# PEER feed-forward on one core: raw-weight ring in spent operand buffers, more GpSimd subtractions, a lighter backlog, and another first expert group

## The chip, the cores and the metric

One core of one Trainium2 chip. The metric is the device time of one execution in microseconds, taken as the median of several runs. Lower is better.

## The reference

Two transformer blocks run one after the other over 256 tokens of width 2048. The first block and the mixer of the second (two kinds of attention with gated branches) are not touched. The change lies in the last part, the product-key feed-forward (PEER):

```python
def peer_ffn(h, w_query, sub_keys, expert_u, expert_v):
    q = (ht @ w_query).reshape(n_tok, PEER_HEADS, 2, HALF_KEY)
    scores = jnp.einsum('thpc,hpnc->thpn', q, sub_keys)
    s1, i1 = lax.top_k(scores[:, :, 0], PEER_TOPK)
    s2, i2 = lax.top_k(scores[:, :, 1], PEER_TOPK)
...
    top_score, pos = lax.top_k(cand_score, PEER_TOPK)
    expert_ids = jnp.take_along_axis(cand_id, pos, axis=-1)
    gates = jax.nn.softmax(top_score, axis=-1)
...
        act = jax.nn.gelu(jnp.einsum('thkd,td->thk', expert_u[idb], xb))
        return jnp.einsum('thk,thkd->td', gb * act, expert_v[idb])
```

There are 8 heads with 16 chosen experts each, out of 128 x 128 = 16384 experts. `h` is `x` after an RMS norm, and a last residual addition and RMS norm follow.

## The kernel before

**Dense products instead of gathers by token.** The kernel multiplies all 256 tokens with all 16384 rows of `expert_u` (the *first expert product*), applies gelu, and multiplies by a gate matrix that is zero where an expert was not chosen. The result, `a`, goes to DRAM (`a_dram`, one row of 256 tokens for each expert). The last stage multiplies `a` with rows of `expert_v`.

**Weight units.** All big products read their weights as 332 *units* of [128, 2048] f32. Units 188 to 203 are the queries' weights (`wq`), units 204 to 331 the first expert product (`uT`), 32 chunks of 4 units. Each unit goes through a pipeline:

- SyncE's queue (SP) issues two loads of [128, 1024] into `raw`, a pool of four such tiles (`load_half`, L102);
- ScalarE rounds a half to `wh` (L111);
- VectorE, or GpSimd for the pairs (unit, half) in the table `POOL_SUB`, computes `wl = raw - wh` (L112);
- TensorE multiplies with `wh` and `wl` (L216 and L217, L213 and L214 for the edges of an accumulation). Two units are half of a chunk, and each half ends in an epilogue that ScalarE starts (L225) and VectorE adds to (L226).

`pump` sets the order: before unit n it records the loads up to unit n + 2 and the splits up to unit n + 1. The `raw` tile of a half comes free when both ScalarE and the engine of the subtraction have read it.

**Side work.** Generators (`side`) are advanced four times in a unit, between the matmuls of the product:

- `topk_a` (L1114 to L1140) makes scores and finds the top 16 on VectorE. Until the gates exist, chunks of the first product are spilled to DRAM (`xs`, L1243); 19 are.
- `g_build` (L1300 to L1329) builds the gate matrix out of one-hot rows `oh`, and writes it to `g_dram`.
- `order_experts` (L1395 to L1494) sorts the experts so that unused ones come together. It makes 16 pairs of one-hot matrices (`ob` L1479, `oa` L1483, both VectorE; `ob` is scaled by ScalarE, L1480) and 128 small matmuls (L1490). Its result is the index `idx` of the gathers in the last stage.
- `backlog` brings the spilled chunks back: a gate load `G` (L1354), a load of the chunk `Xr` (L1359), a multiply on VectorE (L1368) and a write to `a_dram` (L1371) for each chunk, with 6 yields behind it.

**Last stage.** 64 groups of 256 experts are taken in the order `gro`, which starts 55, 14, 37, ... For a group, GpSimd issues two gathers of [128, 2048] from `expert_v` (`v_load`, tiles `vraw`, six of them, L1532) and two of [128, 256] from `a_dram` (`a_load`, `araw`, L1538). `v_split` makes `ah` and `al` from `araw` (L1544, L1545), then `vh` and `vl` (L1552, L1553). The matmuls (L1561 to L1563) stand under conditions on the number of experts used, so a group of unused experts costs TensorE nothing. L1561 runs 648 times in the profiled execution, 8 for each of 81 pairs of a group and a half of the tokens, and the groups are sorted; of the first group, 55, none runs.

The operands of the products live in a pool `hbr` of tiles [128, 2048]: the queries' operand `act3` takes four, the expert product's operand `act4` four more. `act3` is last read by unit 203.

Of the kernel before, what the change touches and what calls it, by code (L numbers as in the profile page):

```python
# [6 lines left out]
F32 = mybir.dt.float32  # L7
F32R = mybir.dt.float32r
# [4 lines left out]
AF = mybir.ActivationFunctionType  # L13
# [33 lines left out]
TB = 32  # L47
GW = 8
GB = 3
POOL_SUB = {(n, 1) for n in [*range(8, 24, 2), *range(36, 64, 2), *range(188, 332, 2)]}  # L50
PRIO = 1000
EPRIO = 6000
OHB = 12
# [12 lines left out]
def model(tc, I, out):  # L66
    nc = tc.nc
    V, S, T, PO = nc.vector, nc.scalar, nc.tensor, nc.gpsimd
    es = ExitStack()
    with es:  # L70
        cpool = es.enter_context(tc.tile_pool(name="cst", bufs=1))
        es_w = es.enter_context(ExitStack())
        rawp = es_w.enter_context(tc.tile_pool(name="raw", bufs=NRAW))
        whp = es_w.enter_context(tc.tile_pool(name="wh", bufs=NWH))
        wlp = es_w.enter_context(tc.tile_pool(name="wl", bufs=NWL))
        hbr = es_w.enter_context(tc.tile_pool(name="hbr", bufs=8))
# [15 lines left out]

        units = []
        raws, splits, hooks = {}, {}, {}
        pos = [0, 0, 0]
        active, waiting = [[], []], [[], []]

        def load_half(n, hf, parts=1):
            f = rawp.tile([128, 1024], F32, name="raw", tag="raw")
            w = units[n][0][:, hf * 1024:(hf + 1) * 1024]  # L100
            for i in range(0, 1024, 1024 // parts):
                nc.sync.dma_start(f[:, i:i + 1024 // parts], w[:, i:i + 1024 // parts])  # L102
            raws.setdefault(n, []).append(f)
# [42 lines left out]
        def pump(upto):  # L146

            while pos[2] < upto:
                n = pos[2]
                while pos[0] < min(len(units), n + 3):  # L150
                    with tc.high_priority(offset=PRIO):
                        load(pos[0])
                    pos[0] += 1
                while pos[1] < min(len(units), n + 2, pos[0]):
                    with tc.high_priority(offset=PRIO):
                        split(pos[1])
                    pos[1] += 1
                units[n][1](splits.pop(n))
                pos[2] += 1
                for f in hooks.pop(pos[2], []):  # L160
                    f()
# [175 lines left out]
        def rB(R, n=4):  # L337
            return R[:, None, 0:256].to_broadcast([128, n, 256])
# [6 lines left out]
        with ExitStack() as b1:  # L345
            w_ = b1.enter_context(tc.tile_pool(name="work1", bufs=1))
# [439 lines left out]
            for u in range(4):  # L786
                t = H("xr")
                xr.append(t)
                if u < 2:
                    f = rawp.tile([128, 1024], F32, name="raw", tag="raw")  # L790
                    h, l = whp.tile([128, 1024], F32R, name="wh"), wlp.tile([128, 1024], F32R, name="wl")
# [89 lines left out]
            late = []  # L881
# [217 lines left out]
        with ExitStack() as bt:  # L1099
# [8 lines left out]

            def q_epi(c):
                def epi(q):  # L1110
                    V.tensor_mul(q, q, rB(R3))
                    for t in range(2):
                        side(topk_a(c, t, q))
                return epi  # L1114

            def topk_a(c, t, q):

                p = sps()
                for j in range(4):
                    hp = c * 4 + j  # L1120
                    T.matmul(p[:, j * 128:j * 128 + 128], q[:, j, t * 128:t * 128 + 128],
                             skT[hp // 8][:, (hp % 8) // 2, (hp % 2) * 128:(hp % 2) * 128 + 128],
                             start=True, stop=True)
                yield
                sc = small("sc", [128, 4, 128], bufs=2)
                sc2 = small("sc2", [128, 4, 128], bufs=SC2)
                S.activation(sc, p.rearrange("p (a b) -> p a b", a=4), AF.Copy)
                yield
                ix = small("ix", [128, 4, 16], bufs=2, dt=U32)
                for j in range(4):  # L1130
                    sv = s12[t][:, c * 4 + j]
                    V.max(sv[:, 0:8], sc[:, j])
                    V.max_index(ix[:, j, 0:8], sv[:, 0:8], sc[:, j])
                    V.match_replace(sc2[:, j], sv[:, 0:8], sc[:, j], -3e38)
                    V.max(sv[:, 8:16], sc2[:, j])
                    V.max_index(ix[:, j, 8:16], sv[:, 8:16], sc2[:, j])
                    yield
                V.tensor_copy(x12[t][:, c * 4:c * 4 + 4], ix)
                done.append((c, t))
                if sum(1 for d in done if d[1] == t) == 4:  # L1140
                    side(topk_b(t))
                yield
# [125 lines left out]
                gemm(I["wq"][c], act3, 4, q_epi(c))  # L1268
            side(scaled())
            n = len(units) + 1  # L1270
            for c in range(NS):
                gemm(I["uT"][c], act4, 4, u_epi(c), parts=c == NS - 1)
            while len(ready) < 2:
# [100 lines left out]
        def backlog(sets):  # L1374
            for i, c in enumerate(sets):
                if i == 0:
                    load_g(c)
                    load_x(c)
                yield
                if i + 1 < len(sets):  # L1380
                    load_g(sets[i + 1])
                    load_x(sets[i + 1])
                make_a(c)
                for _ in range(6):
                    yield

        def order_experts():
# [131 lines left out]
        NV = 12  # L1519
        NGR = NT // KG  # L1520
        gro = [(i * 23 + 55) % NGR for i in range(NGR)]
        raw, ar, sv, sa = {}, {}, {}, {}

        def ix(i, kk):
# [3 lines left out]
        def v_load(i):  # L1528
            raw[i] = []
            for kk in range(KG):  # L1530
                f = w_.tile([128, 2048], F32, name="vraw", tag="vraw", bufs=6)
                PO.indirect_dma_start(f, None, I["v"], ix(i, kk))  # L1532
                raw[i].append(f)

        def a_load(i):
            ar[i] = w_.tile([128, KG, 256], F32, name="araw", tag="araw", bufs=4)
            for kk in range(KG):
                PO.indirect_dma_start(ar[i][:, kk], None, arow, ix(i, kk))  # L1538

        def v_split(i):  # L1540
            h = w_.tile([128, KG, 256], F32R, name="ah", tag="ah", bufs=3)
            l = w_.tile([128, KG, 256], F32R, name="al", tag="al", bufs=3)
            f = ar.pop(i)
            S.activation(h, f, AF.Copy)  # L1544
            V.tensor_sub(l, f, h.bitcast(F32))  # L1545
            sa[i] = (h, l)
            sv[i] = []
            for f in raw.pop(i):
                for hf in range(2):
                    q = slice(hf * 1024, hf * 1024 + 1024)  # L1550
                    h, l = (w_.tile([128, 1024], F32R, name=n, tag=n, bufs=NV) for n in ("vh", "vl"))
                    S.activation(h, f[:, q], AF.Copy)  # L1552
                    V.tensor_sub(l, f[:, q], h.bitcast(F32))  # L1553
                    sv[i].append((h, l))

        def v_mm(i, t, last=False):
            ah, al = (x[:, :, t * 128:t * 128 + 128] for x in sa[i])
# [17 lines left out]
        es_d.enter_context(order_)  # L1575
        for i in range(3):
            v_load(i)
            a_load(i)
        s1, e0, e1 = (T.value_load(bnd[0:1, i:i + 1], min_val=0, max_val=NT * 128) for i in range(3))
        for i in range(2):  # L1580
            v_split(i)
        v_load(3)
        a_load(3)
        for i in range(NGR):
# [151 lines left out]
```

## Time and profile before

| | us |
|---|---|
| median of 3 runs | 2651.11 (2650.2 to 2661.93) |
| the profiled execution's own time | 2651.99 |
| its span | 2650.2 |
| TensorE busy | 2546.2 (96%) |
| VectorE busy | 1947.1 (73%) |
| ScalarE busy | 1492.9 (56%) |
| GpSimd busy | 662.7 (25%) |

The shares are means over the whole program, and its stages differ: units 188 to 203 run from about 1220 to 1310 us, the first expert product from there to 2150, and the last stage from 2150 to the end. The granted clock of TensorE was 0.987 over the span. The profile of the chain that ended last is of no help in this program: TensorE is almost always the one that ends last, and what matters is where it stands still.

### The profile page before, as it was taken

Reading aid. Unit: us, or ns where it says so; the run is one execution under the profiler, and the core shown is the slowest. Engines: PE = TensorE matmul, PEld = TensorE weight load, DVE = VectorE, ACT = ScalarE, POOL = GpSimd, SP = SyncE. Lnnn points to the kernel's source line nnn. Section 1 sums busy time; section 2 is a strip of 40 time slices with the busy share of each in tenths; the row PEclk is TensorE's granted clock in tenths of the full one; section 3 lists DMA queues with packets and bytes.
Section 4 is the critical chain, followed back from the end, with each engine's and each line's share of the span. In section 5 each row is a group of like instructions: output and inputs, shape, how many; then the busy total and the mean of one; then the engine's idle time right before and its main releaser. Section 6 shows DMA issues by size and latency. Waiting matters only on the chain. (4 is left out here: it accounts for less than half of the span.)

```text
span 2650.2 us, 38662 instructions
## 1 busy us (share of the span) xinstructions
PE 2546.2 (96%) x14650; PEld 2166.0 (82%) x14650; DVE 1947.1 (73%) x2691; ACT 1492.9 (56%) x2179; POOL 662.7 (25%) x401
## 2 busy tenths in 40 slices
PE   8999999999999999999998999999799989999998
PEld 7878878888888888888887788888687867777776
DVE  7988877675555655767999888888975447767776
ACT  7666665555544544555455777664453446656565
POOL 0440111000000000001214221221211248667773
PEclk9999999999999999999999999999899989999999
DMA  6454424554555455555555677778799769898885
GB/s 226 154 170 154 158 97 137 201 179 158 175 169 173 165 185 185 188 190 192 175 184 175 214 232 233 231 234 299 264 353 347 239 237 360 305 330 317 320 311 209
DMA packets 173397, 584.81 MB, mean 221 GB/s; under 512 B 17424, under 2 KB 50704, under 8 KB 156688
## 3 DMA queue, kind: packets, MB, share of 16 engines
q1 hardware_dynamic: 114192, 411.88, 45.5%
q0 software_dynamic: 24576, 151.01, 15.6%
q10 hardware_dynamic: 34432, 19.27, 2.5%
q8 instruction: 126, 2.06, 0.3%
q14 instruction: 71, 0.58, 0.1%
HBM read 536.48 MB, written 45.61 MB: 220 GB/s over the span
## 5 line engine op out<-in xcount | busy, mean ns | idle before, releaser
L216 PE MATMUL acc<-a,wh 128*128 128x512 f32 x3120 | 1121.6, 401 | 3.6 <-ACT wh L111 2.7
L111 ACT ACTIVATE wh<-raw 128x1024 fp32r<-128x1024 f32 x662 | 696.7, 1056 | 481.8 <-PE acc L216 256.8
L112 DVE TENSOR_TENSOR wl<-raw,wh 128x1024 fp32r<-128x1024 f32 x568 | 722.0, 1275 | 300.0 <-ACT wh L111 296.7
L217 PE MATMUL acc<-a,wl 128*128 128x256 f32 x3120 | 886.5, 284 | 26.9 <-DVE wl L112 15.2
L216 PEld LDWEIGHTS acc<-a,wh 128*128 128x128 f32 x3120 | 590.4, 189 | 135.3 <-ACT wh L111 4.3
L112 POOL TENSOR_TENSOR wl<-raw,wh 128x1024 fp32r<-128x1024 f32 x94 | 268.6, 2857 | 1692.4 <-ACT wh L111 1634.8
L217 PEld LDWEIGHTS acc<-a,wl 128*128 128x128 f32 x3120 | 594.8, 191 | 37.6 <-DVE wl L112 19.9
L1553 DVE TENSOR_TENSOR vl<-vraw,vh 128x1024 fp32r<-128x1024 f32 x256 | 296.5, 1220 | 14.9 <-ACT vh L1552 14.4
L1561 PE MATMUL o<-vh,ah 128*128 128x512 f32 x648 | 257.3, 397 | 28.8 <-ACT vh L1552 11.9
L216 PE MATMUL acc<-ax,wh 128*128 128x512 f32 x720 | 266.4, 407 | 10.6 <-ACT wh L800 6.5
L1562 PE MATMUL o<-vl,ah 128*128 128x512 f32 x648 | 253.5, 391 | 0.5 <-DVE vl L1553 0.5
L1563 PE MATMUL o<-vh,al 128*128 128x512 f32 x648 | 253.2, 391 | 0.0
L1552 ACT ACTIVATE vh<-vraw 128x1024 fp32r<-128x1024 f32 x256 | 248.9, 1044 | 0.0
L225 ACT ACTIVATE y<-acc 128x512 f32<-128x512 f32 x162 | 96.0, 593 | 226.0 <-PE acc L214 224.1
L217 PE MATMUL acc<-ax,wl 128*128 128x256 f32 x720 | 209.7, 291 | 5.2 <-DVE wl L112 3.0
L226 DVE TENSOR_TENSOR y<-y,acc 128x512 f32<-128x512 f32 x162 | 110.6, 683 | 128.4 <-ACT y L225 127.8
L1532 POOL DMA_INDIRECT vraw<-in_v_dram,idx x128 | 165.1, 1290 | 86.5 <-DVE vl L1553 50.7
L1538 POOL DMA_INDIRECT araw<-a_dram,idx x128 | 174.6, 1364 | 48.2 <-issue 36.9
L1561 PEld LDWEIGHTS o<-vh,ah 128*128 128x128 f32 x648 | 122.2, 189 | 68.4 <-issue 26.7
L216 PEld LDWEIGHTS acc<-ax,wh 128*128 128x128 f32 x720 | 138.9, 193 | 40.2 <-ACT wh L800 6.5
L217 PEld LDWEIGHTS acc<-ax,wl 128*128 128x128 f32 x720 | 139.6, 194 | 8.9 <-DVE wl L112 3.9
L1544 ACT ACTIVATE ah<-araw 128x512 fp32r<-128x512 f32 x64 | 40.3, 629 | 188.9 <-PE o L1562 139.6
(508 smaller groups left out, 3716.6 us busy)
## 6 DMA issues: line engine op xcount, KB each, us to landing
raw<-in_w_dram SPq DMA_DIRECT2D x278, 512.0 KB, 4.2
raw<-in_uT_dram SPq DMA_DIRECT2D x256, 512.0 KB, 4.9
raw<-in_wo_dram SPq DMA_DIRECT2D x64, 512.0 KB, 4.4
raw<-in_wq_dram SPq DMA_DIRECT2D x32, 512.0 KB, 4.2
g_dram<-gst ACTq DMA_DIRECT2D x32, 512.0 KB, 7.7
G<-g_dram SPq DMA_DIRECT2D x32, 512.0 KB, 7.3
xs<-y SPq DMA_DIRECT2D x19, 512.0 KB, 4.5
Xr<-xs SPq DMA_DIRECT2D x19, 512.0 KB, 9.9
```

What stands on the lines that cost most here:

```text
L111: S.activation(h[:, q], f[:, q], AF.Copy)
L112: (PO if (n, hf) in POOL_SUB else V).tensor_sub(l[:, q], f[:, q], h[:, q].bitcast(F32))
L216: T.matmul(acc[:, j], wh[:, js], xx, start=f, stop=False)
L217: T.matmul(acc[:, j, 0], wl[:, js], xx[:, 0], start=False, stop=False)
L226: V.tensor_add(y, y, acc[:, :, 0])
L1532: PO.indirect_dma_start(f, None, I["v"], ix(i, kk))
L1538: PO.indirect_dma_start(ar[i][:, kk], None, arow, ix(i, kk))
L1552: S.activation(h, f[:, q], AF.Copy)
L1553: V.tensor_sub(l, f[:, q], h.bitcast(F32))
L1561: T.matmul(ps[t][d], ah[:, kk], wh, start=False, stop=False)
L1562: T.matmul(ps[t][d], ah[:, kk], wl, start=False, stop=False)
L1563: T.matmul(ps[t][d], al[:, kk], wh, start=False, stop=stop)
```

## The change

It has six parts. In the changed file the lines stand 6 to 12 further down.

1. From unit 208 on, the raw weights go to four tiles of a whole unit each, out of `hbr` (`ring`, the tiles of `act3`), and the loads run up to unit n + 4.
2. `POOL_SUB` gets the second halves of the odd units 189 to 223 as well: 18 more subtractions on GpSimd instead of VectorE.
3. The queries' scale `R3`, a VectorE multiply in each of four epilogues (L1111), becomes the scale of the ScalarE copy of the scores (L1127).
4. `backlog` yields 7 times behind a chunk instead of 6.
5. `gro[0]` and `gro[7]` change places: group 24 is now the first, group 55 the eighth.
6. In the last stage the first three `v_load` are issued ahead of the first three `a_load`, and the first group's `ah` and `al` are made behind its `vh` and `vl`.

```diff
-POOL_SUB = {(n, 1) for n in [*range(8, 24, 2), *range(36, 64, 2), *range(188, 332, 2)]}
+POOL_SUB = {(n, 1) for n in [*range(8, 24, 2), *range(36, 64, 2), *range(188, 224), *range(224, 332, 2)]}
...
         def load_half(n, hf, parts=1):
-            f = rawp.tile([128, 1024], F32, name="raw", tag="raw")
+            if ring and n >= ring[0]:
+                if len(ring) == 1:
+                    ring.extend(hbr.tile([128, 2048], F32, name="ring", tag="hbr") for _ in range(4))
+                f = ring[1 + n % 4][:, hf * 1024:(hf + 1) * 1024]
+            else:
+                f = rawp.tile([128, 1024], F32, name="raw", tag="raw")
...
-                while pos[0] < min(len(units), n + 3):
+                while pos[0] < min(len(units), n + (5 if len(ring) > 1 else 3)):
...
                 def epi(q):
-                    V.tensor_mul(q, q, rB(R3))
...
-                S.activation(sc, p.rearrange("p (a b) -> p a b", a=4), AF.Copy)
+                S.activation(sc, p.rearrange("p (a b) -> p a b", a=4), AF.Copy, scale=R3[:, 256 + t:257 + t])
...
             n = len(units) + 1
+            ring.append(len(units) + 4)
...
                 make_a(c)
-                for _ in range(6):
+                for _ in range(7):
                     yield
...
         gro = [(i * 23 + 55) % NGR for i in range(NGR)]
+        gro[0], gro[7] = gro[7], gro[0]
...
         for i in range(3):
             v_load(i)
+        for i in range(3):
             a_load(i)
...
         for i in range(2):
-            v_split(i)
+            v_split(i, late=i == 0)
```

On SyncE's queue, where the first expert product's loads begin, this stood before (`raw` are the half tiles, `xs` the spilled chunks):

```order
L102 DMA raw<-in_wq_dram 128x1024 x32
L102 DMA raw<-in_uT_dram 128x1024 x15
L1243 DMA xs_13235<-y 128x1024
L102 DMA raw<-in_uT_dram 128x1024 x8
L1243 DMA xs_13496<-y 128x1024
```

and this stands there now:

```order
L108 DMA raw<-in_wq_dram 128x1024 x32
L108 DMA raw<-in_uT_dram 128x1024 x3
L108 DMA ring<-in_uT_dram 128x1024 x2
L108 DMA raw<-in_uT_dram 128x1024 x2
L108 DMA ring<-in_uT_dram 128x1024 x4
L108 DMA raw<-in_uT_dram 128x1024 x2
L108 DMA ring<-in_uT_dram 128x1024 x2
L108 DMA raw<-in_uT_dram 128x1024
L108 DMA ring<-in_uT_dram 128x1024 x4
L1248 DMA xs_13235<-y 128x1024
L108 DMA ring<-in_uT_dram 128x1024 x8
```

The first loads into the ring have moved ahead of five of the eight halves of units 204 to 207 on the same queue, and they need the matmuls of the last query units to be done. From there on each load goes to a ring tile, up to two units earlier than before.

On VectorE, in the stretch of `order_experts`, this stood before (unit 289 and the next ones; `ob` and `oa` are the one-hots, `y<-y,acc` is an epilogue):

```order
L112 TENSOR_TENSOR wl<-raw,wh 128x1024
L1479 TENSOR_TENSOR ob<-cst,pf 128x1024
L1483 TENSOR_TENSOR oa<-cst,pf 128x1024
L1479 TENSOR_TENSOR ob<-cst,pf 128x1024
L1483 TENSOR_TENSOR oa<-cst,pf 128x1024
L1468 CAST jf<-ji 128x128
L112 TENSOR_TENSOR wl<-raw,wh 128x1024
L226 TENSOR_TENSOR y<-y,acc 128x512
```

and this stands at the beginning of the one-hots now (unit 293 and the next ones; L1374 is the backlog's multiply):

```order
L1485 TENSOR_TENSOR ob<-cst,pf 128x1024
L1489 TENSOR_TENSOR oa<-cst,pf 128x1024
L118 TENSOR_TENSOR wl<-ring,wh 128x1024
L232 TENSOR_TENSOR y<-y,acc 128x512
L118 TENSOR_TENSOR wl<-ring,wh 128x1024 x2
L1485 TENSOR_TENSOR ob<-cst,pf 128x1024
L1489 TENSOR_TENSOR oa<-cst,pf 128x1024
L118 TENSOR_TENSOR wl<-ring,wh 128x1024
L232 TENSOR_TENSOR y<-y,acc 128x512
L118 TENSOR_TENSOR wl<-ring,wh 128x1024
L1374 TENSOR_TENSOR y<-y,G 128x8x4x32
L118 TENSOR_TENSOR wl<-ring,wh 128x1024
```

Before, one to three pairs stand between two `wl`; now a pair is followed by two to four `wl`. Between the first and the last pair there stood 10 `wl` and 3 epilogues of VectorE before (units 289 to 297), and there stand 29 `wl` and 10 epilogues now (units 292 to 312).

On GpSimd, at the beginning of the last stage, this stood before:

```order
L112 TENSOR_TENSOR wl<-raw,wh 128x1024 x55
L1532 DMA vraw<-in_v_dram,idx 128x2048 x2
L1538 DMA araw<-a_dram,idx 128x256 x2
L1532 DMA vraw<-in_v_dram,idx 128x2048 x2
L1538 DMA araw<-a_dram,idx 128x256 x2
```

and this stands there now:

```order
L118 TENSOR_TENSOR wl<-ring,wh 128x1024 x3
L1202 TENSOR_TENSOR eq<-eq,x_1_11870 128x2048
L118 TENSOR_TENSOR wl<-ring,wh 128x1024 x59
L1539 DMA vraw<-in_v_dram,idx 128x2048 x6
L1545 DMA araw<-a_dram,idx 128x256 x6
```

All six gathers of the first three groups' `vraw` have moved ahead of the first gather of `araw`.

## Rows read from the trace of the kernel before

**Rows 1.** Busy us (instructions) of PE, PEld, DVE, ACT, POOL by stretch; PEclk; DMA share; GB/s.

```profile
1362.00:1432.00 70.00, 60.38 (x330) 50.95 (x329) 69.64 (x150) 32.08 (x37) 21.83 (x7) 0.98 0.51 168
1432.00:1518.00 86.00, 81.91 (x521) 67.50 (x520) 78.97 (x91) 60.53 (x125) 27.45 (x7) 0.96 0.65 210
1834.00:1950.00 116.00, 99.01 (x595) 82.40 (x595) 107.85 (x125) 55.39 (x58) 27.72 (x7) 0.93 0.82 294
1950.00:2004.00 54.00, 54.00 (x313) 47.32 (x312) 31.24 (x27) 23.16 (x25) 9.60 (x4) 1.00 0.99 378
2004.00:2060.00 56.00, 49.68 (x270) 42.15 (x270) 30.57 (x25) 22.85 (x26) 12.02 (x5) 0.97 0.88 329
2150.00:2176.00 26.00, 13.63 (x78) 11.77 (x79) 13.71 (x14) 12.10 (x16) 16.79 (x15) 0.74 0.71 266
2176.00:2600.00 424.00, 407.83 (x1759) 327.34 (x1758) 309.43 (x293) 257.62 (x292) 312.14 (x234) 1.00 0.89 325
```

**Rows 2.** Waits of TensorE, 1362 to 1432: who for whom, us in total, times, longest.

```profile
PE acc L217 <- DVE wl L112: 9.6, 6, 3.1
```

**Rows 3.** Waits of TensorE, then of ScalarE, 1432 to 1518.

```profile
PE s L1318 <- ACT oh L1306: 3.5, 2, 2.3
...
ACT wh L111 <- DMA raw<-in_uT_dram: 7.3, 2, 6.3
```

**Rows 4.** Waits of TensorE, then of ScalarE, 1834 to 1950.

```profile
PE acc L217 <- DVE wl L112: 5.6, 6, 2.0
PE acc L217 <- POOL wl L112: 5.0, 1, 5.0
PE s L1490 <- ACT ob L1480: 3.8, 3, 1.9
...
ACT wh L111 <- DMA raw<-in_uT_dram: 32.1, 13, 7.8
```

**Rows 5.** Waits of TensorE, 2004 to 2060.

```profile
PE acc L217 <- POOL wl L112: 5.7, 4, 2.0
```

**Rows 6.** ScalarE's start of two epilogues that follow each other: start, duration, wait.

```profile
2081.64 0.60 ACT L225 ACTIVATE y<-acc 128x512 f32<-128x512 f32 x1 [1.89 <-PE acc L214]
...
2092.94 0.60 ACT L225 ACTIVATE y<-acc 128x512 f32<-128x512 f32 x1 [1.83 <-PE acc L214]
```

**Rows 7.** VectorE's groups, 1834 to 1950: busy, mean ns, idle before.

```profile
L1479 DVE TENSOR_TENSOR ob<-cst,pf 128x1024 f16<-128x1024 f32 x16 | 23.1, 1442 | 3.4 <-PE s L1490 3.4
L1483 DVE TENSOR_TENSOR oa<-cst,pf 128x1024 f16<-128x1024 f32 x16 | 19.4, 1213 | 0.0
```

**Rows 8.** GpSimd's subtractions: 1240 to 1450 (ns min/median/max), then the two longest later ones.

```profile
L112 POOL TENSOR_TENSOR wl<-raw,wh x16: 2380/2506/6672, 1248.4 to 1438.3; 128x1024 fp32r<-128x1024 f32 x16
...
1482.24 8.47 POOL L112 TENSOR_TENSOR wl<-raw,wh 128x1024 fp32r<-128x1024 f32 x1 [14.41 <-ACT wh L111]
...
1873.32 11.77 POOL L112 TENSOR_TENSOR wl<-raw,wh 128x1024 fp32r<-128x1024 f32 x1 [11.03 <-ACT wh L111]
```

**Rows 9.** VectorE's subtractions, 1240 to 1450 and 2060 to 2150; the query scale.

```profile
L112 DVE TENSOR_TENSOR wl<-raw,wh 128x1024 fp32r<-128x1024 f32 x51 | 74.1, 1462 | 2.7 <-ACT wh L111 2.6
...
L112 DVE TENSOR_TENSOR wl<-raw,wh 128x1024 fp32r<-128x1024 f32 x22 | 26.9, 1224 | 36.0 <-ACT wh L111 36.0
...
L1111 DVE TENSOR_TENSOR y<-y,R x4: 1209/1218/1226, 1265.0 to 1328.1; 128x1024 f32<-128x1024 f32 x4
```

**Rows 10.** Waits of TensorE, 1254 to 1362.

```profile
PE acc L216 <- DVE y L226: 0.8, 1, 0.8
```

**Rows 11.** Timeline, 2140 to 2172: start, duration, engine, instruction, idle before.

```profile
2154.95 0.95 POOL L1538 DMA_INDIRECT araw<-a_dram,idx  x1 [9.46 <-DMA a_dram<-y]
...
2159.95 0.95 POOL L1538 DMA_INDIRECT araw<-a_dram,idx  x1 [0.31 <-issue]
...
2167.68 0.63 ACT L1544 ACTIVATE ah<-araw 128x512 fp32r<-128x512 f32 x1 [3.50 <-DMA araw<-a_dram,idx]
...
2169.31 0.79 PE L1561 MATMUL o<-vh,ah 128*128 128x512 f32 x1 [11.09 <-ACT vh L1552]
```

More of the change, by code (lines that the diff above doesn't have):

```diff
@@ L94, in model @@
         raws, splits, hooks = {}, {}, {}
+        ring = []
         pos = [0, 0, 0]
@@ L1538, in a_load, with v_split, a_split @@
                 PO.indirect_dma_start(ar[i][:, kk], None, arow, ix(i, kk))
-        def v_split(i):
+        def v_split(i, late=False):
             h = w_.tile([128, KG, 256], F32R, name="ah", tag="ah", bufs=3)
             l = w_.tile([128, KG, 256], F32R, name="al", tag="al", bufs=3)
-            f = ar.pop(i)
-            S.activation(h, f, AF.Copy)
-            V.tensor_sub(l, f, h.bitcast(F32))
             sa[i] = (h, l)
             sv[i] = []
+            def a_split():
+                f = ar.pop(i)
+                S.activation(h, f, AF.Copy)
+                V.tensor_sub(l, f, h.bitcast(F32))
+            if not late:
+                a_split()
             for f in raw.pop(i):
@@ L1550, in v_split @@
                     q = slice(hf * 1024, hf * 1024 + 1024)
[L1551 to L1554, printed above, removed]
+                    wh, wl = (w_.tile([128, 1024], F32R, name=n, tag=n, bufs=NV) for n in ("vh", "vl"))
+                    S.activation(wh, f[:, q], AF.Copy)
+                    V.tensor_sub(wl, f[:, q], wh.bitcast(F32))
+                    sv[i].append((wh, wl))
+            if late:
+                a_split()
         def v_mm(i, t, last=False):
```

## The prediction

> **What bounds the kernel now.** The totals name TensorE, which is busy for 96% of the span, so I looked only for the stretches in which it stands still, and cut the second block at these with the view of busy time by stretch [rows 1]. Between them TensorE has next to nothing to give. For each stretch I then read what ended TensorE's waits and, one step back, what ended the waits of the engine it waited for.
>
> - **A, 1362 to 1432** (top-k beside the first units of the expert product). VectorE is busy 69.64 of 70 us and is the bound. TensorE is idle 9.6 us, all of it waiting for VectorE's `wl` [rows 1, 2].
> - **A2, 1432 to 1518** (gate matrix). TensorE is idle 4.1 us, of which 3.5 for a one-hot of ScalarE. ScalarE had itself waited for a raw half for 6.3 us [rows 1, 3]. Just ahead of that a GpSimd subtraction had taken 8.47 us instead of the usual 2.5 and had held its raw tile that long [rows 8].
> - **B, 1834 to 1950** (ordering of the experts). TensorE is idle 17.0 us and runs at a mean granted clock of 0.93 [rows 1]. Its waits are for `wl` of VectorE, for one `wl` of GpSimd that took 11.77 us, and for `ob` [rows 4, 8]. VectorE, 107.85 of 116 us busy, spends 42.5 of them on the 16 pairs of `ob` and `oa` [rows 1, 7]. ScalarE waits 32.1 us for raw halves, in 13 pieces [rows 4].
> - **C, 1950 to 2060** (backlog). At first the DMA engines are busy to 0.99 at 378 GB/s and TensorE just holds. Then TensorE loses 6.3 us, 5.7 of them for `wl` of GpSimd: the margin that the loads had was used up [rows 1, 5].
> - **D, 2150 to 2176** (start of the last stage). TensorE waits 11.09 us until its first product at 2169.31. The clock stands at 0.74 over the stretch [rows 1, 11].
> - From 2176 to 2600 TensorE is busy 407.83 of 424 us: nothing to gain [rows 1].
>
> A time saved in A to D moves the end by as much, since TensorE bounds what follows.
>
> **Query scale.** Four multiplies of 1.218 us leave VectorE, 4.9 us [rows 9]. They stand between 1265 and 1328, where TensorE waits 0.8 us in all [rows 10]. The copy that takes the scale over exists already. Worth 0 (0 to -0.8).
>
> **18 more subtractions on GpSimd.** Each takes one of about 1.22 us from VectorE, the time that it has where GpSimd is quiet [rows 9]. But beside GpSimd's 16 subtractions of 1240 to 1450 VectorE's own took 1.462 us at the mean instead of 1.224: 51 x 0.238 = 12.1 us, or 0.76 for each of the 16 [rows 8, 9]. VectorE's other instructions were stretched too; the highest that one can cost is the 2.5 us that it lasts [rows 8]. I take 1.1, nearer to the row than to the bound, since `wl` is VectorE's commonest work there. Then the exchange gains 0.1 us each. Ten of the 18 lie in units 203 to 221, in and just ahead of A: -1 there, with bounds of +13 (10 x (2.5 - 1.22)) and -4.6 (10 x (1.22 - 0.76)).
>
> The trace shows a partial stretch of VectorE, not a standstill. The Trainium skill ("SBUF — State Buffer", section "Who interferes with whom") says that a VectorE instruction with two inputs from SBUF contends with a GpSimd instruction that reads SBUF, and that whoever loses the shared port is fully blocked; with this every moved subtraction could hold VectorE for its whole length, and the sum would have the +13 just named. The 0.76 speaks against that as the usual case, the 8.47 and 11.77 us of GpSimd show it the other way round.
>
> **The ring.** It adds 4 MB of raw buffers and two units of lead, some 11 us, since two units take 2092.94 - 2081.64 = 11.30 us [rows 6]. Its first loads wait for the last query units' matmuls, with five halves of units 204 to 207 behind them on SyncE's queue. These halves are wanted a unit later (5.65 us), and TensorE waits for nothing there now; I take 0, with +3 as the upper bound, about half a unit. In A a longer lead doesn't help, as VectorE is the bound there. In A2 it covers ScalarE's 6.3 us, which is less than 11: **-3.5** for the one-hot, which was late by what ScalarE had lost (0 to -4.1). In B it takes away most of the raw waits. A and A2 together, with the rest of the last part: -1 - 3.5, of which I count **-4** (bounds -18, all idle time of both stretches and some of the clock, and +12).
>
> **Seven yields, and where the ordering now stands.** The one-hots cost VectorE the same 42.5 us [rows 7]. Before, up to three pairs, some 8 us, stand between two `wl`; with the new order one pair, 2.66 us, is followed by two to four `wl`, and the 16 pairs stretch over 20 units rather than 9. In one unit VectorE then has at most one pair, 1.5 subtractions (1.9 us) and about one multiply (1.2 us) on the average with the epilogue, some 6 us at the worst against 5.65, and less as soon as there is a unit without a pair. So VectorE no longer bounds, the runs that starve GpSimd's `wl` become shorter, and with the ring the raw tile of a slow one holds nobody up. I take the three waits of [rows 4] to go to a fifth of themselves: -11.5 of 14.4. With the idle time goes some of the slow clock: 0.07 x 99 is 6.9 us at most, and I take a third, -2.5 [rows 1]. **B: -14** (0 to -23.9, the idle 17.0 and all of the clock).
>
> Each backlog chunk moves three times 0.52 MB (G, Xr, the write to `a_dram`). With seven advances at four in a unit that is 1.57 MB in 9.9 us, with eight 11.3 us: 159 against 139 GB/s, next to 186 for the weights (1.05 MB in 5.65 us). So 345 becomes 325 where 378 was moved [rows 1]. The ordering's own traffic is on top. The lead kept through this stretch is up to two units longer, so the 6.3 us and 0.03 x 50 = 1.5 us of clock in C should mostly go. **C: -6** (0 to -7.8).
>
> **The last stage.** With a used group first, TensorE needs the first group's operands and no longer the second's. Its `vraw` gathers now stand ahead of all `araw`, and the first can go before the product's end. `araw` still cannot be issued before `a_dram` is written, 2154.95 [rows 11]. What it meets then is new: four of the six `vraw` gathers wait for buffers until the last matmuls, about 2150, and stand ahead of it, 4.2 MB. At the 378 GB/s of the fullest stretch [rows 1] that is 11.1 us, and the 0.26 MB of `araw` 0.7, to about 2162. In the trace the second `araw`, issued at 2159.95 behind two younger `vraw`, was there at 2167.68, 7.7 us later [rows 11]; 2154.95 + 7.7 = 2162.65 agrees. With the 1.63 from the start of `ah` to the first product it is 2164.3 instead of 2169.31 [rows 11]: **D: -5** (0 if `araw` is as late as before; -11.1 if the whole wait goes).
>
> The Trainium skill ("DMA: Bandwidth & Descriptors", under "Queues, rings and completion order") has rings that are worked through in order, with round robin between queues only; by it `araw` stands behind the whole 4.2 MB. By it the term stays -5; the 7.7 us agree.
>
> **Sum.** -4 - 14 - 6 - 5 = -29 from the profiled execution's 2651.99, which lies 0.9 above the median of the runs: 2623 in either reading.
>
> **Rivals.**
> 1. *Starved GpSimd (slower).* A GpSimd subtraction beside a dense run of VectorE can take 8 to 12 us, and cost TensorE 5.0 once [rows 4, 8]. In A VectorE is dense. If each new one that is starved costs 5.0, six of the 18 use up the 29 us; ten cost 50, and the time is 2623 + 50 = 2673. Against it: of 16 in this stretch the median is 2.5 us and the longest 6.7 [rows 8]. Chance 0.06.
> 2. *Ordering is only moved.* The ordering now reaches into units 298 to 312, where the DMA engines were busy to 0.99 [rows 1]. If B's time is lost there, only A2, C in part and D are left: 2652 - 4 - 3 - 5 = 2640. For it: there is no slack for TensorE at 378 GB/s. Chance 0.15.
> 3. *The ring doesn't do what it is there for.* A lead needs bandwidth to be built up; where the DMA engines are full it stays as short as before, and C keeps its 7.8 us: 2629. Chance 0.17.
> 4. *VectorE held for whole subtractions.* The +13 in A instead of -1, so 2623 + 14 = 2637; what speaks against it is the mean of 1.462 [rows 9]. Chance 0.07.
> 5. *All stalls go.* -18 - 23.9 - 7.8 - 11.1 = -60.8: 2591; with most of it, 2600. Chance 0.12.
>
> **How the numbers follow.** My forecast of 2623, with its own range of 2611 to 2632, has the rest, 0.43. The range of 8 in 10 leaves out the far half of rival 5 and rival 1: 2600 to 2645. Half a per cent, 13 us, is about what a measurement of this kernel can tell from no change: faster ends at 2638, slower begins at 2664. Faster: my forecast, rivals 3 and 5, half of 4 and a fifth of 2, 0.78; slower: rival 1 with a little for what I have not seen, 0.07; the rest, 0.15, is the same.
>
> **What would show it.** A2: no raw wait of ScalarE above 3 us at 1432 to 1518, and no wait for `oh`. A: TensorE idle about as before, GpSimd busier, VectorE's `wl` still about 1.45 us. B: TensorE idle under 6 us between the first and last `ob`, with ScalarE's 32.1 us for raw under 10. C: no waits for GpSimd's `wl`, with a mean rate no higher than 378. D: first product 14 us behind the end of the expert product instead of 19, with a wait for `ah`. The prediction is wrong if GpSimd's subtractions above 6 us are many, if new waits for raw show at 1306 to 1330, if the one-hot stretch still has TensorE waiting for `ob`, or if the last stage, which started earlier, waits for `vraw` later on.

## The result, and the profile after

The changed kernel takes 2619.81 us (median of 4 runs, 2618.66 to 2623.14) against 2656.28 (4 runs, 2650.2 to 2661.93) for the kernel before: a ratio of 0.9865, with a 95% interval of 0.9835 to 0.9896. The profiled execution took 2623.14 with a span of 2621.4, which is 28.8 us below the 2650.2 of the kernel before; the forecast was 29. That the two agree so closely owes something to the execution that was profiled: the kernel before has two runs near 2651 us and two near 2662, and the profiled one (2651.99) is like the faster two; between the medians lie 36.5 us. And the parts of that sum did not come out as forecast.

To see where the time went I cut both traces at the starts of ScalarE's epilogues (L225 before, L231 after). They come once in each half of a chunk, in the same order in both kernels. I count from the one at about 1207 us; the 75th is the last of the expert product.

| stretch (epilogues) | before | after | difference |
|---|---|---|---|
| up to the 13th (queries and the first units) | 1351.2 | 1353.2 | +2.0 |
| 13th to 33rd (top-k and gate matrix: A, A2) | 265.1 | 266.9 | +1.8 |
| 33rd to 50th | 206.4 | 206.4 | 0.0 |
| 50th to 75th (ordering and backlog: B, C, and what follows) | 326.8 | 299.5 | -27.3 |
| 75th to the first product of the last stage (D) | 19.9 | 16.6 | -3.3 |
| from there to the end | 480.9 | 478.8 | -2.1 |

Nearly all of it came from the ordering and the backlog. This is the busy time by stretch of the changed kernel, in the columns of [rows 1], from the 50th epilogue to the 58th and from there to the 67th:

```profile
1826.47:1923.93 97.46, 94.29 (x552) 80.61 (x551) 92.58 (x114) 48.71 (x52) 28.40 (x8) 1.00 0.98 369
1923.93:2035.57 111.64, 109.01 (x681) 94.41 (x680) 87.57 (x73) 56.70 (x60) 25.79 (x9) 0.98 0.94 341
```

and this is the kernel before between the same epilogues:

```profile
1822.60:1949.86 127.26, 110.27 (x657) 92.10 (x657) 117.74 (x138) 58.98 (x62) 30.14 (x8) 0.93 0.83 300
1949.86:2059.04 109.18, 102.86 (x575) 88.76 (x574) 61.06 (x50) 45.19 (x50) 21.62 (x9) 0.98 0.94 354
```

The first row lost 29.8 us, the second gained 2.5. The counts of matmuls say why the two must be taken together: 105 fewer stand in the first now and 106 more in the second, since the ordering moved. Over both, TensorE's idle time fell from 23.3 to 5.8 us, and its busy time from 213.1 to 203.3, with 1232 and 1233 matmuls: that is the granted clock, 0.93 before and 1.00 now in the first row. The DMA engines were at 0.83 in it before, and are at 0.98 now.

The waits of TensorE (another of 0.5 us follows) and of ScalarE in the first of these stretches, changed kernel, answer to [rows 4]:

```profile
PE acc L223 <- POOL wl L118: 2.7, 1, 2.7
...
```

```profile
ACT wh L117 <- PE acc L222: 27.0, 16, 3.4
...
ACT wh L117 <- DMA ring<-in_uT_dram: 1.7, 1, 1.7
```

ScalarE waited 32.1 us for raw halves, and now waits 1.7; it waits for TensorE to give back `wh` tiles, as it should where TensorE is the bound. One step further back, SyncE's queue shows what the loads themselves waited for, first before and then now, between the 50th and 58th epilogues: it is the subtraction that still read their tile, 53.7 us in all before, and 20.7 now.

```profile
SPq L102 <- DVE wl L112: 31.5, 13, 11.1
SPq L102 <- POOL wl L112: 22.2, 6, 9.3
```

```profile
SPq L108 <- POOL wl L118: 14.3, 4, 8.4
...
SPq L108 <- DVE wl L118: 6.4, 6, 2.9
```

The last stage, changed kernel, answers to [rows 11] (start, duration, engine, instruction, idle time before it):

```profile
2125.97 0.94 POOL L1539 DMA_INDIRECT vraw<-in_v_dram,idx  x1 [3.97 <-PE acc L220]
...
2137.46 1.05 POOL L1545 DMA_INDIRECT araw<-a_dram,idx  x1 [6.74 <-DMA a_dram<-y]
...
2141.87 0.63 ACT L1555 ACTIVATE ah<-araw 128x512 fp32r<-128x512 f32 x1 [10.14 <-DMA araw<-a_dram,idx]
...
2142.55 0.79 PE L1575 MATMUL o<-vh,ah 128*128 128x512 f32 x1 [7.80 <-ACT ah L1555]
```

The write of `a_dram` used to release the first gather 5.5 us behind the last epilogue (at 2149.44), and now does so 11.5 behind it (at 2125.97). The row of DMA issues from 2126 to 2152, with the KB of one and the median us to landing, has the reason:

```profile
a_dram<-y SPq DMA_DIRECT2D x1, 256.0 KB, 8.0
```

Three `vraw` gathers were issued in the 2.7 us ahead of it and a fourth 1.1 us behind it, and their 4.2 MB share the engines with this write. The same holds in all eight kernels of this document with the reordered gathers, where the write lands after 7.7 to 8.3 us; in the six others it lands after 2.0. The gather of `araw` itself then takes 4.4 us. TensorE waits for `ah` where it had waited for `vh`.

### The profile page after: what moved, and what is told of

Same layout as the page of the kernel before. It is cut to its first block, busy times and chain, and to the rows that moved or that the text cites. A ratio compares the mean times of both kernels' runs of the same rounds, so it can differ in the third digit from the quotient of the medians.

```text
span 2621.4 us, 38683 instructions
## 1 busy us (share of the span) xinstructions
PE 2534.1 (97%) x14650; PEld 2158.6 (82%) x14650; DVE 1936.4 (74%) x2669; ACT 1491.0 (57%) x2177; POOL 707.9 (27%) x419
## 5 line engine op out<-in xcount | busy, mean ns | idle before, releaser
L118 DVE TENSOR_TENSOR wl<-raw,wh 128x1024 fp32r<-128x1024 f32 x372 | 462.7, 1245 | 232.5 <-ACT wh L117 229.5
L117 ACT ACTIVATE wh<-raw 128x1024 fp32r<-128x1024 f32 x414 | 437.3, 1058 | 311.7 <-PE acc L222 191.8
L223 PEld LDWEIGHTS acc<-a,wl 128*128 128x128 f32 x3120 | 591.5, 190 | 27.3 <-DVE wl L118 16.6
L118 POOL TENSOR_TENSOR wl<-raw,wh 128x1024 fp32r<-128x1024 f32 x42 | 113.0, 2691 | 1078.9 <-ACT wh L117 1035.9
L118 POOL TENSOR_TENSOR wl<-ring,wh 128x1024 fp32r<-128x1024 f32 x70 | 204.7, 2924 | 546.5 <-ACT wh L117 528.3
L117 ACT ACTIVATE wh<-ring 128x1024 fp32r<-128x1024 f32 x248 | 259.9, 1054 | 144.6 <-PE acc L222 102.4
L118 DVE TENSOR_TENSOR wl<-ring,wh 128x1024 fp32r<-128x1024 f32 x178 | 234.3, 1323 | 58.8 <-ACT wh L117 58.7
L231 ACT ACTIVATE y<-acc 128x512 f32<-128x512 f32 x162 | 96.0, 593 | 212.7 <-PE acc L220 201.1
L1539 POOL DMA_INDIRECT vraw<-in_v_dram,idx x128 | 157.2, 1228 | 87.4 <-DVE vl L1565 47.8
L1575 PEld LDWEIGHTS o<-vh,ah 128*128 128x128 f32 x648 | 122.0, 188 | 65.0 <-issue 27.3
```

The costliest lines, as they stand in the source:

```text
L117: S.activation(h[:, q], f[:, q], AF.Copy)
L118: (PO if (n, hf) in POOL_SUB else V).tensor_sub(l[:, q], f[:, q], h[:, q].bitcast(F32))
L223: T.matmul(acc[:, j, 0], wl[:, js], xx[:, 0], start=False, stop=False)
L1575: T.matmul(ps[t][d], ah[:, kk], wh, start=False, stop=False)
```

## The experiments

Two theories stood at first. Theory 1: the ring alone brings the gain. This rests on the order of the built programs: with the ring alone VectorE's one-hot pairs are already spread over 29 `wl`, and with seven yields alone they stay packed over 10, as before (both with their first and last pair as ends). Theory 2 is the prediction's: the yields and the new order relieve the stretch, and the ring covers late raw halves. Kernels told together below were timed together, on one chip. Stretches are those of one profiled execution each.

**The ring alone, the subtractions alone, the yields alone, the old start.**

```diff
 # ring_only: before, with load_half as in the change, and with
+            ring.append(len(units) + 4)
+                while pos[0] < min(len(units), n + (5 if len(ring) > 1 else 3)):
 # subs_only: before, with
+POOL_SUB = {(n, 1) for n in [..., *range(188, 224), *range(224, 332, 2)]}
 # yields_only: before, with
+                for _ in range(7):
 # old_start: the changed kernel, with
-        gro[0], gro[7] = gro[7], gro[0]
         for i in range(3):
             v_load(i)
-        for i in range(3):
             a_load(i)
-            v_split(i, late=i == 0)
+            v_split(i)
```

The first three also have the query scale on ScalarE, and the rest as before.

> The kernel before with the ring of raw buffers alone. Theory 1: the ring brings the gain of the ordering stretch by itself, since with it the one-hot pairs already stand as in the changed kernel (29 wl between the first and last pair instead of 10); 22 to 30 us faster than before, nearly all of it between the epilogues that stood at 1834 and 1950. Theory 2, as the prediction has it: the seven yields relieve that stretch and the ring only covers late raw halves; 4 to 10 us faster, with one-hot waits of TensorE left in the ordering stretch.

> The kernel before with the 18 more GpSimd subtractions alone. Theory 1: VectorE gains nothing in the top-k stretch from the exchange and the runs get slower there: 3 to 12 us slower between 1340 and 1530, nothing elsewhere. Theory 2, as the prediction has it: about 1 us faster, in the noise.

> The kernel before with seven yields instead of six behind a chunk of the backlog, alone. Theory 1: the one-hot pairs stand as before (10 wl between first and last), so the ordering stretch stays as it is; 0 to 5 us faster, from the backlog stretch behind 1950. Theory 2, as the prediction has it: 12 to 18 us faster, most of it in the ordering stretch.

> The changed kernel with the last stage started as before: group 55 first, araw gathers between the vraw gathers, ah and al first. Both theories: 5 us slower than the changed kernel (about 24 us faster than before), with the first product of the last stage 19 to 20 us behind the last epilogue of the expert product instead of 16.6. If the start is worth nothing by itself, the time is that of the changed kernel.

Measured, as ratios to the kernel before: the ring alone 2618.36 us, 0.9848 (0.9822 to 0.9875); the subtractions alone 2652.63, 0.9979 (0.9962 to 0.9997); the yields alone 2650.97, 0.9971 (0.9951 to 0.999); the changed kernel with the old start 2627.19, 0.9881 (0.9851 to 0.9912). The ring alone has the whole gain of the change. The kernels with the subtractions and with the yields are a few us faster each, on intervals that nearly reach 1; what these few us are stays open. Both also have the query scale, which no run has alone. Waits of ScalarE, first with the ring alone (1818 to 1920), then with the yields alone (1824 to 1959):

```profile
ACT wh L117 <- DMA ring<-in_uT_dram: 5.4, 3, 1.9
```

```profile
ACT wh L117 <- DMA raw<-in_uT_dram: 41.8, 16, 10.9
```

A lighter backlog leaves raw halves as late as they were: from the 50th to the 67th epilogue it takes 209.4 us with the ring alone and 239.5 with the yields alone (whose profiled execution, 2657.66, was its slowest), 236.4 before. With the old start the first product comes 20.0 us behind the last epilogue, as both theories had it. Its median is 7.4 us above the changed kernel's, which wasn't timed beside it, and its four runs range over 8.3 us, so that the 5 us of the theories are neither shown nor ruled out.

**The changed kernel without one part, or with the lead taken back.**

```diff
 # old_subs
-POOL_SUB = {... *range(188, 224), *range(224, 332, 2)]}
+POOL_SUB = {... *range(188, 332, 2)]}
 # six_yields
-                for _ in range(7):
+                for _ in range(6):
 # ring_no_lead
-                while pos[0] < min(len(units), n + (5 if len(ring) > 1 else 3)):
+                while pos[0] < min(len(units), n + 3):
 # ring_start_scale: old_subs and six_yields together
```

> The changed kernel without the 18 more GpSimd subtractions. Theory 1, they cost time where VectorE bounds: the stretch between the epilogues at 1353 and 1455 gets 5 to 8 us shorter, 2 to 3 us of it come back as time lost up to 1620, the total is 3 to 6 us below the changed kernel (2614 to 2617). Theory 2, the exchange is even, as the prediction has it: within 2 us of the changed kernel, and that stretch within 2 us of 102.

> The changed kernel with six yields instead of seven in the backlog. Theory 1, the ring carries the ordering and backlog stretches and the lighter backlog only moves time between them: both stretches together within 3 us of the changed kernel's 209.1. Theory 2, the lighter backlog is needed for the gain: 8 to 14 us slower, with ScalarE waiting for raw halves again.

> The changed kernel with the ring's four unit tiles, but the loads recorded up to unit n + 2 as before; VectorE's order of one-hots and subtractions is that of the changed kernel. Theory 1a, the lead of the loads brings the gain: ScalarE waits 15 us or more for raw halves in the ordering stretch and the two stretches take 220 to 235 us instead of 209. Theory 1b, it is the order on VectorE, and that a slow subtraction no longer holds a tile that the next load needs: 207 to 213 us, the time within 3 us of the changed kernel.

> The changed kernel without the 18 subtractions and with six yields: ring, query scale on ScalarE and the new start of the last stage are left. Theory 1: these carry all of the gain, so 2612 to 2616, some 5 us below the changed kernel and 4 to 5 below the ring alone. Theory 2, every part adds its share: 5 to 12 us above the changed kernel.

Measured: 2620.22 (2618.52 to 2622.97), 2615.52 (2613.69 to 2616.81), 2619.14 (2618.48 to 2622.91) and 2615.55 (2613.92 to 2617.45); against the kernel before 0.9874 (0.9844 to 0.9904), 0.9852 (0.9822 to 0.9881), 0.9871 (0.9841 to 0.9901) and 0.9851 (0.9821 to 0.988).

- The subtractions are even on the total: 2620.22 without them against 2619.14 for the changed kernel in its repeat (`ring_no_lead`), and 2615.55 against 2615.52 with six yields. So theory 1's 3 to 6 us fell. Between the 13th and 33rd epilogues the five kernels with them and with four ring tiles take 260.5 to 266.9 us (mean 263.3), the four ring kernels without them 262.6 to 263.6 (mean 263.0). The stretch that theory 1 named did get shorter without them, 102.0 to 93.7, but it is not the same work: VectorE had done more of the gate matrix by then, and it came back later. Ahead of it the subtractions do cost something: from the 1st to the 13th epilogue all eight kernels with them take 145.7 to 145.8 us, and the five with the query scale but without them 143.6 to 143.7. In the changed kernel a matmul of the scores waits 1.3 us there for an epilogue of VectorE, a wait that the changed kernel without them doesn't have.
- Six yields are better than seven by 4.7 us on the same chip (`ring_start_scale` against `old_subs`, which differ in nothing else). Theory 1's bound of 3 us on the two stretches holds, 206.4 against 209.1, but it had not said that seven are the worse choice.
- `ring_no_lead` tells nothing on the lead. Its instructions stand in the same order on every engine as those of the changed kernel: loads run ahead as far as tiles are free, whatever n they are recorded at. It is a repeat, and a measure of the noise: spans of 2616.7 and 2621.4, up to 3 us in one stretch.

What the seventh yield costs is seen in the changed kernel's timelines of VectorE and, below it, of GpSimd:

```profile
2000.48 1.23 DVE L1485 TENSOR_TENSOR ob<-cst,pf 128x1024 f16<-128x1024 f32 x1 [2.04 <-PE s L1496]
2001.62 1.22 DVE L1489 TENSOR_TENSOR oa<-cst,pf 128x1024 f16<-128x1024 f32 x1
2002.76 1.22 DVE L1485 TENSOR_TENSOR ob<-cst,pf 128x1024 f16<-128x1024 f32 x1
2003.89 1.22 DVE L1489 TENSOR_TENSOR oa<-cst,pf 128x1024 f16<-128x1024 f32 x1
2005.03 3.37 DVE L118 TENSOR_TENSOR wl<-ring,wh 128x1024 fp32r<-128x1024 f32 x1
```

```profile
2003.92 3.40 POOL L118 TENSOR_TENSOR wl<-ring,wh 128x1024 fp32r<-128x1024 f32 x1 [10.24 <-ACT wh L117]
```

and TensorE's:

```profile
2008.45 0.39 PE L223 MATMUL acc<-a,wl 128*128 128x256 f32 x1 [2.63 <-DVE wl L118]
```

Two pairs stand together, a `wl` behind them is stretched to 3.37 us beside a subtraction of GpSimd, TensorE waits 2.63 us, and the 5 us behind that have a mean granted clock of 0.66 (columns as in [rows 1]), part of them at 2.4 GHz and part at 1.2: a matmul with `wh` takes 0.39 us at first and 0.63 from 2009.96 to 2012.09.

```profile
2008.00:2013.00 5.00, 4.55 (x21) 3.78 (x22) 4.94 (x5) 1.39 (x2) 0.00 (x0) 0.66 0.67 228
```

With six yields this place has one pair, and the stretch from the 58th to the 67th epilogue takes 107.3 us with no wait of TensorE at all, against 111.6. All three kernels with four ring tiles and six yields have this 107.3, and all five with seven have 111.6 or 111.7.

**Fewer tiles, the swap without the reordered gathers, fewer yields.**

```diff
 # ring_of_three (and ring_of_two, with 2)
-                while pos[0] < min(len(units), n + (5 if len(ring) > 1 else 3)):
+                while pos[0] < min(len(units), n + 3):
-                    ring.extend(hbr.tile(...) for _ in range(4))
-                f = ring[1 + n % 4][...]
+                    ring.extend(hbr.tile(...) for _ in range(3))
+                f = ring[1 + n % 3][...]
 # swap_only: as old_start, but this line stays
         gro[0], gro[7] = gro[7], gro[0]
 # ring_start_five: as ring_start_scale, with
+                for _ in range(5):
```

> The changed kernel with three ring tiles instead of four and loads recorded up to unit n + 2. On VectorE the first 12 one-hot pairs stand packed, with 9 wl between them, nearly as in the kernel before. Theory 1a, raw buffers are what counts: the ordering and backlog stretches together take 209 to 216 us, ScalarE's waits for raw halves stay under 15 us. Theory 1b, the order on VectorE is what counts: 225 us or more, with waits of TensorE for wl and ob as before.

> The changed kernel with two ring tiles, as much raw space as before, and loads recorded up to unit n + 2; the one-hot pairs stand packed as before. Theories 1a and 1b: the two stretches take about the 236 us of the kernel before (228 to 240), ScalarE waits over 25 us for raw halves, the total is 18 us or more above the changed kernel; what the other parts are worth without buffers is the rest, 0 to 10 us faster than before. If the other parts were the gain, it would stay within 5 us of the changed kernel.

> The changed kernel with the swapped first group, but araw gathers between the vraw gathers and ah and al first, as before. Theory 1, the used first group is the gain and the araw gathers, with fewer bytes ahead of them, come sooner: the first product of the last stage 13 to 15 us behind the last epilogue instead of 16.6, the total the same or 2 us faster. Theory 2, the order of the gathers is needed, because GpSimd otherwise stands at the first araw with the later vraw behind it: 18 to 20 us, and 2 to 4 us slower.

> Ring, query scale and new start with the subtractions as before and five yields in the backlog. Theory 1, the ring carries a denser backlog too and the end of the program's second-to-last stage only gets freer: 0 to 5 us below the 2615.5 of the kernel with six. Theory 2, the DMA engines are full at six already and a denser backlog makes raw halves late: 3 to 10 us above it, with ScalarE waiting for raw halves at 0.99 DMA share.

Measured: 2629.56, 0.9909 (0.9875 to 0.9942); 2659.91, 1.0025 (1.0008 to 1.0042); 2619.65, 0.9874 (0.984 to 0.9907); 2626.89, 0.9897 (0.9863 to 0.9931).

With two tiles, as much raw space as before, the ring and all five other parts together are no faster than the kernel before, by the median 0.25% slower. ScalarE's waits, 1829 to 1967, with two tiles, and 1819 to 2035, with three:

```profile
ACT wh L117 <- DMA ring<-in_uT_dram: 46.9, 13, 15.3
```

```profile
ACT wh L117 <- DMA ring<-in_uT_dram: 9.9, 4, 3.9
```

The two stretches take 241.8 us with two tiles, 216.2 with three, and 209.1 with four. With three, VectorE still has the first 12 pairs packed, and TensorE still waits for `ob`, 4.6 us. So space for raw weights is the larger part: the step from two tiles to three, with the first 12 pairs packed in both (the last four are spread over 20 `wl` with three), is 25.6 of the 32.7 us between two tiles and four here. Behind the 67th epilogue three tiles lose 6.0 us again, with TensorE waiting 3.4 us for `wl` of GpSimd, so that it is 19.4 of 32.4 up to the 75th; by the medians it is 30.4 of some 40 us. The 216.2 stands at the edge of what theory 1a allowed, and the wait for `ob` says that the order is worth something too. The two weren't set wholly apart, since the order comes out of the same scheduler that sees the tiles.

The swap alone starts the last stage best. Its timeline, for comparison with the one above (last epilogue at 2122.66):

```profile
2128.17 0.95 POOL L1545 DMA_INDIRECT araw<-a_dram,idx  x1 [9.46 <-DMA a_dram<-y]
...
2132.23 0.63 ACT L1555 ACTIVATE ah<-araw 128x512 fp32r<-128x512 f32 x1 [7.59 <-DMA araw<-a_dram,idx]
...
2133.86 0.50 PE L1575 MATMUL o<-vh,ah 128*128 128x512 f32 x1 [2.42 <-ACT vh L1564]
```

Here the same write lands in 2.0 us, 5.5 behind the last epilogue, the gather in 4.1, and the first product runs 11.2 us behind the epilogue: 8.7 better than before, of which the reordered gathers of the change give back 5.4. The median, 2619.65, doesn't show these 5 us against the changed kernel's 2619.81; its profiled execution, 2615.71, does. The two weren't timed together, so that on the total this stays unproven.

Five yields are about 11 us worse than six (0.9897 against 0.9851, timed on different chips; the stretch from the 50th to the 75th epilogue is 11.5 us longer). ScalarE does not wait for raw halves any more than with six; TensorE waits 5.5 us for `ob`, for which it does not wait at all with six, and 4.1 for a `wl` of GpSimd (2.9 with six), with the clock at 0.87 from 1960 to 2000. So neither theory had the reason: the waits are those of the ordering, not of the DMA engines.

| kernel | 13th to 33rd | 50th to 75th | 75th to first product | span |
|---|---|---|---|---|
| before | 265.1 | 326.8 | 19.9 | 2650.2 |
| changed | 266.9 | 299.5 | 16.6 | 2621.4 |
| ring_only | 263.6 | 299.8 | 19.2 | 2617.1 |
| subs_only | 264.9 | 319.6 | 19.7 | 2643.4 |
| yields_only | 265.8 | 331.3 | 19.8 | 2655.8 |
| old_start | 262.9 | 299.7 | 20.0 | 2622.8 |
| old_subs | 263.3 | 301.6 | 16.5 | 2616.8 |
| ring_no_lead | 265.1 | 301.1 | 16.6 | 2616.7 |
| ring_start_scale | 262.7 | 296.7 | 16.6 | 2615.6 |
| ring_start_five | 262.6 | 308.2 | 16.7 | 2624.7 |
| six_yields | 260.8 | 296.8 | 16.6 | 2614.1 |
| ring_of_three | 260.6 | 312.5 | 16.5 | 2628.2 |
| ring_of_two | 268.8 | 331.9 | 16.5 | 2656.9 |
| swap_only | 260.5 | 300.8 | 11.2 | 2613.8 |

The best kernels run are six_yields and ring_start_scale, 2615.5 us, 4 below the changed kernel and its repeat. Six yields with the swap alone wasn't run.

## Why the prediction was right

The total was right, 2623 against 2619.81, and within its range; of its terms the small ones came near, and of the larger ones two missed in opposite directions. That the sum still hit is luck.

- **Query scale, 0.** From the 1st to the 13th epilogue the kernel before takes 144.2 us, and the five kernels with the scale but without the extra subtractions 143.6 to 143.7. That is about -0.5, on one execution of the kernel before, and lies within the bounds of 0 to -0.8.
- **18 subtractions, -1.** Even on the total and between the 13th and 33rd epilogues (263.3 against 263.0 us), so right within the noise where the term was worked out, for ten of the 18. Seven of the others lie in the queries' units, where the prediction had nothing for them: there they cost 2.0 us, nearly all of it between the 7th and 8th epilogues (14.5 us against 12.5). With the scale's -0.5 and 0.4 us from ahead of the 1st epilogue this makes the +2.0 in the first row of the table of stretches. VectorE's `wl` between the 13th and 20th epilogues took 1.58 us at the mean with them and 1.79 without. GpSimd's own subtractions did get longer between the 13th and 20th epilogues, a median of 3.10 us against 2.41 without the extra ones. The rule of the Trainium skill ("SBUF — State Buffer", "Who interferes with whom") that the loser is fully blocked is not contradicted by this, but the +13 that the prediction drew from it did not come.
- **A and A2, -4.** +1.8 in the profiled execution, -1.8 as the mean of the five kernels with four ring tiles and the subtractions. The raw wait of ScalarE is gone, as forecast; but TensorE still waits 3.5 us for `oh`, of which 2.5 are for one that VectorE makes. Mis-sized by some 2 us, which is no more than the noise.
- **B and C, -14 and -6.** Measured -27.3 for both. The failed step is the one headed "Seven yields, and where the ordering now stands": it gave the new order to the seven yields and had of the ring that it "takes away most of the raw waits". The runs show that the ring brings both the raw halves and the order, and that the seven yields are worth nothing with it (six are 4.7 us faster) and do not bring the gain without it (239.5 us; 0.9971 on the total). The step, like the section on the change, had also read the new order as more even than it is: the first three pairs have no `wl` between them, and at two later places two pairs stand together, the last of which is the 2.63 us above. The sum was too small by its clock: of the -20, some 16 were idle time (measured 17.5) and 4 were clock, where busy time fell by 9.8 for the same number of matmuls. The 27.3 are of one pair of executions; the kernels without more raw space differ among themselves by 12 us between the 50th and the 75th epilogue (319.6 to 331.9), so a few us of it are noise. The sign of C as a stretch by itself was wrong (+2.5), as ten of the 16 pairs of one-hots and 104 of the ordering's 128 matmuls now stand in it, which is rival 2 in a small way.
- **Rivals 2 and 3** put the DMA engines' 0.99 against the gain. They don't bind: at 0.98 and 369 GB/s TensorE runs at full clock. The 0.83 of the kernel before between the 50th and 58th epilogues was the loads waiting for tiles (53.7 us on SyncE's queue), not a need that was met.
- **D, -5.** 3.3 us to the first product, and 2.1 behind it; of the latter 0.9 is left at the mean of the eight kernels with the reordered gathers (479.4 from the first product to the end) against the five with the old start (480.3). I had the `araw` gather issued at the old distance and queued behind 4.2 MB for 7.7 us; in fact it is issued 6 us later, as it is the `a_dram` write that the 4.2 MB delay (8.0 us to landing against 2.0), and then takes 4.4. So the size was about right, and the mechanism was not: the contention falls on the write that the gather waits for, and the run without the new order of gathers shows that it is avoidable.
- **Rival 1** did not come: the longest of GpSimd's subtractions up to the 33rd epilogue is 9.72 us, and TensorE waits 1.9 us for them in all between the 13th and the 33rd.

So the total was right, while B and C gained 7 us more than forecast, and A and A2 with what lies ahead of them 8 less: two misses that cancelled.

## What to carry to other kernels

Where an engine waits for loads and the DMA engines are at 0.8, look for what a load waits for before one looks for bandwidth: here it was a tile that a late subtraction held, and room for two more units, with the order that came with it, was worth some 27 us. A kernel whose order comes from a scheduler must be built with each part of a change alone, because one part can move work that the text of another seems to move. When gathers are put ahead of a smaller one to save their wait, count the bytes that they put beside the write on which the smaller one depends.

## What the runs showed of the hardware

- The run-to-run spread went with the raw buffers. The kernel before and the three others without more raw space ranged over 10 to 15 us in 10 to 19 runs each (2650.1 to 2664.8, 2644.8 to 2658.7, 2644.4 to 2657.7, 2655.7 to 2666.1); the kernels with three or four tiles ranged over 1.5 to 8.3 in 4 runs each, against 11.7 in the 4 runs of the kernel before that stand beside the changed kernel's. Why was not tried.
- The granted clock fell to a mean of 0.66 in the 5 us behind a wait of only 2.63 us, and the stretch around it was 4.3 us longer than with six yields, of which the wait is 2.6.
- Beside gathers of 4.2 MB a write of 256 KB to DRAM took 7.7 to 8.3 us to land in eight kernels, against 2.0 in the six without such gathers beside it.
